# Product-key experts on one core: the gathered block is selected first and its rows are fetched from there, 56 of 128 first products run ahead

## The chip, the cores and the metric

The kernel runs on one core of one Trainium2 chip. A core has a matrix engine (PE, with its weight loads, PEld), a vector engine (DVE), a scalar engine (ACT), a GpSimd engine (POOL) and DMA queues, one of them fed by SyncE (SP). The metric is the device time of one execution in microseconds (us).

## The reference

The program is two transformer blocks over 512 tokens of 1024 features in float32. The part that the change touches is the feed-forward of the first block, with product keys and 16384 experts. Cut to what matters:

```python
def peer_ffn(h, w_query, sub_keys, expert_u, expert_v):
    # per token and head (8 heads): two 128-wide queries
    q = h @ w_query                              # 1024 -> 8 x 2 x 128
    s = q . sub_keys                             # 128 scores for each half
    (v1, i1), (v2, i2) = top16(s[0]), top16(s[1])
    best, pos = top16(v1[:, None] + v2[None, :]) # 16 of the 256 pairs
    gate = softmax(best); expert = i1 * 128 + i2
    # 8 heads x 16 = 128 experts of each token
    y = sum_e gate_e * gelu(h . expert_u[e]) * expert_v[e]
```

## The kernel before, in words

The 512 tokens are four blocks of 128. **Block 0 is gathered**: for each of its 128 (head, pick) slots one indirect DMA from POOL brings the 128 rows of `peer_u` that the 128 tokens picked (`g_row`, 128 x 1024, 512 KB, three buffers), and DVE forms the dot products (L889); then 128 such rows of `peer_v` are added up with the weights `dots` (L894). That makes 256 rows in all. **Blocks 1 to 3 (384 tokens) are dense**: all 16384 experts are computed in 128 chunks of 128. A chunk has a *first product* (`hp`: 24 matmuls 128x384 of `peer_uT`, then a gelu into `act`), a weighting with the gates `gt`, and a *second product* (`o`: 18 matmuls 128x512 with `peer_v`, added up in PSUM over all chunks). Every weight tile is 128x1024 in float32 and goes through `split`: a DMA on SP's queue (`w_raw`), a rounding copy on ACT (`w_hi`) and the difference on DVE or POOL (`w_lo`, L108), with five buffers (`WB`); each product then takes three matmul passes.

The gates of a dense block come in three steps. `scores` multiplies with 16 tiles of `w_query` (24 matmuls 128x256 for a pair of blocks) and with the sub-keys (L735, 128x128 matmuls in float32), and takes the 16 best of 128 for each (`top16`: five DVE operations L745 to L749 with their value loads). `select` finds the 16 best pairs and their expert numbers on DVE (sums `cs`, 16 more `top16` of 50, comparisons of 128x2048 float16 `ge` and `pr`). `gates` turns them into a dense table by matmuls of one-hots: for 16 tokens at a time DVE writes two `onehot` and two `gated` tiles (128x2048 float16, L853, L854, two buffers each) with `TI` tokens innermost, PE multiplies them token by token (L860, L861: 32 matmuls 128x128, whose operands have a stride of `TI` elements), ACT evicts to `stage`, and a DMA stores them in `gd`. One such step of 16 tokens is called a *G step* here; a block has eight.

The order of the program: scores of blocks 2 and 3, scores of blocks 0 and 1, ten first products (`ahead(10)`), then for blocks 2, 3, 1 a `select` and eight G steps, each with one first product behind it until `PRE` = 32 are there; then the `select` of block 0; and then 128 iterations of second products, of which the first 96 (*doubles*) compute one more first product and the last 32 (*singles*) none. The rows of block 0 are fetched in iterations 5 to 119, in proportion to the work of an iteration, each held until the matmuls of the iteration before are done. First products made ahead split on POOL, the others on DVE. A scheduler orders each engine's instructions within these dependences, so the order on an engine differs from the program's text; each engine runs its own list strictly in order.

The second block of the model follows and isn't touched.

Of the kernel before, what the change touches and what calls it, by code (L numbers as in the profile page):

```python
# [32 lines left out]
SKIP = 5  # L33
LAST = 8
PRE = 32
# [3 lines left out]
TI = 4  # L39
# [45 lines left out]
class Body:  # L85
# [516 lines left out]
    def peer(self, gp, er):  # L602

        nc, tc, A = self.nc, self.tc, self.A
        with ExitStack() as es:
            pool = es.enter_context(tc.tile_pool(name="peer", bufs=1, reuse_waits="tile"))
            wpool = es.enter_context(tc.tile_pool(name="w2", bufs=1, reuse_waits="tile"))
            psh = es.enter_context(tc.tile_pool(name="psh", bufs=2, space=PSUM, reuse_waits="tile"))
# [10 lines left out]
            with tc.tile_pool(name="p2a", bufs=1, reuse_waits="tile") as pa:  # L619
                self.normal(hi, lo, pa, psg)  # L620
                er.close()
                pb = eb.enter_context(tc.tile_pool(name="p2b", bufs=1, side="right", reuse_waits="tile"))
                self.select_tables(pb)
                self.scores(hi, lo, tvs, tis, pa, wpool, psm, psg)
            pact = es.enter_context(tc.tile_pool(name="acts", bufs=1, reuse_waits="tile"))
            act = {}

            def first_product(i, eng=None):
# [6 lines left out]
                act[i] = pact.tile([P, TD], F32, name="act", bufs=PRE + 2)  # L635
                nc.scalar.activation(act[i], ps, AF.Gelu)  # L636
# [12 lines left out]
            nc.vector.scalar_tensor_tensor(slots[:, 0], ij[:, 0], float(P), ij[:, 1], op0=OP.mult, op1=OP.add)  # L649
            nc.vector.tensor_copy(slots[:, 1], g)  # L650
            eb.close()
            with ExitStack() as ec:
# [3 lines left out]
                self.x = None  # L656
                rows = self.gather(slots[:, 0], slots[:, 1], pc)
                next(rows)
                pace = [2 if i + PRE < NE else 1 for i in range(NE)]
                for i in range(NE):  # L660
# [3 lines left out]
                    if i + PRE < NE:  # L664
                        first_product(i + PRE)
                    src = A["peer_v"][i * P:(i + 1) * P, :].rearrange("p (r d) -> p r d", r=1)
                    vh, vl = self.split(src, wpool, WB, None, 1)
                    w = act.pop(i)
# [6 lines left out]
                    for b in range(3):  # L675
                        sl = slice(b * P, (b + 1) * P)
                        for s_, m_ in ((wh, vh), (wh, vl), (wl, vh)):
                            for n in range(2):
                                last = nc.tensor.matmul(out[b][n], s_[:, sl], m_[:, n * 512:(n + 1) * 512],  # L679
                                                 start=i == 0 and m_ is vh and s_ is wh,  # L680
                                                 stop=i == NE - 1 and s_ is wl)
                    if i == NE - PRE + 4:
                        self.keep(gp)
                    if SKIP <= i < NE - LAST:
                        rows.send((2 * P * sum(pace[SKIP:i + 1]) // sum(pace[SKIP:NE - LAST]), mm))
                    mm = last
                for b in range(3):
                    for n in range(2):
                        xs = self.x[b + 1][:, n * 512:(n + 1) * 512]
                        nc.vector.tensor_tensor(xs, xs, out[b][n], op=OP.add)  # L690
# [24 lines left out]
    def scores(self, hi, lo, tvs, tis, pool, wpool, psm, psg):  # L715
        nc, A = self.nc, self.A
        sk = pool.tile([P, 16, P], F32, name="skT")
        nc.sync.dma_start(sk, A["sub_keysT"])
        for first in (2, 0):
# [451 lines left out]
```

## Time and profile before

| what | value |
|---|---|
| time, median of 3 runs | 2060.81 us (2060.49 to 2061.16) |
| the profiled execution: its time, its span | 2068.49 us, 2066.7 us |
| PE busy | 1940.7 us, 94% of the span |
| DVE busy | 1428.8 us, 69% |
| ACT busy | 886.0 us, 43% |
| POOL busy | 639.8 us, 31% |
| mean granted clock of PE | 0.973 of full speed |
| DMA | 402.90 MB, 195 GB/s over the span |

Busy time is the union of an engine's instructions. Matmuls are pipelined: a record of one is longer than the distance to the next, so what a matmul costs is read from the starts of successive ones. Times in the rows are microseconds from the start of the span, "mean ns" is that of one instruction, and "x" is a count. The program's stages in this span: first mixers to 410, normalisation to 428, scores to 541, ten first products to 608, gates of three blocks to 817, second products from 833 to 1748, second block to the end.

### The profile page before, as it was taken

What the parts mean: (1) busy time and instruction counts of PE and PEld (TensorE: products, weight loads), DVE (VectorE), ACT (ScalarE), POOL (GpSimd) and SP (SyncE); (2) the same over time, 40 slices, a digit from 0 to 9 for tenths busy, and PEclk for the clock granted to TensorE, in tenths of its full rate; (3) what the DMA queues carried; (4) which work ended last, traced back from release to release, by engine and by line L of the source; (5) the groups of instructions that cost most, each with busy time, mean ns of one, the idle gap of its engine ahead of it and who ended that gap; (6) DMA issues with size and microseconds to landing.
All of it is one profiled execution on the core that took longest, in us unless ns stands there. A gap on an engine that the chain in (4) does not pass through costs nothing.

```text
span 2066.7 us, 30059 instructions
## 1 busy us (share of the span) xinstructions
PE 1940.7 (94%) x11393; PEld 1760.8 (85%) x11393; DVE 1428.8 (69%) x2662; ACT 886.0 (43%) x1373; POOL 639.8 (31%) x459
## 2 busy tenths in 40 slices
PE   7999988998779999999999999999999999999998
PEld 6778777998779899899999999999999777779998
DVE  3486976379998866778777777877778675443563
ACT  4564745254437666333333333333333334343352
POOL 4334233075452230144333434343333341000000
PEclk9999999999899999999999999999999999999999
DMA  4211014354224445999888988988988775342211
GB/s 163 69 62 50 33 42 143 123 164 133 92 92 180 177 163 222 313 314 335 304 306 308 316 310 284 337 315 302 313 297 291 272 270 196 103 136 74 82 62 52
DMA packets 150354, 402.90 MB, mean 195 GB/s; under 512 B 11584, under 2 KB 60736, under 8 KB 147008
## 3 DMA queue, kind: packets, MB, share of 16 engines
q1 hardware_dynamic: 112768, 264.64, 38.2%
q0 software_dynamic: 36864, 134.23, 18.0%
q8 instruction: 89, 1.46, 0.3%
q10 hardware_dynamic: 576, 2.10, 0.3%
q14 instruction: 57, 0.47, 0.1%
HBM read 371.05 MB, written 29.88 MB: 194 GB/s over the span
## 4 chain that ended last, share of the span: by engine, by line
PE 59%; DVE 12%; DMA 5%; issue 3%; POOL 1%; ACT 1%; DVEq 0%; POOLq 0%; ACTq 0%
PE o L679 21%; PE hp L634 7%; PE hp L633 7%; PE hp L632 7%; DMA g_row<-peer_v,idx 3%; PE mm L121 2%; PE mm L122 2%; PE mm L123 2%; PE mm L133 2%; PE mm L132 2%; PE mm L131 2%; DVE gated L854 1%; PE g L860 1%; PE mm L861 1%; PE g L861 1%
## 5 line engine op out<-in xcount | busy, mean ns | idle before, releaser
L107 ACT ACTIVATE w_hi<-w_raw 128x1024 fp32r<-128x1024 f32 x366 | 385.8, 1059 | 576.5 <-PE hp L633 168.8
L108 DVE TENSOR_TENSOR w_lo<-w_raw,w_hi 128x1024 fp32r<-128x1024 f32 x268 | 326.3, 1219 | 101.2 <-ACT w_hi L107 100.8
L632 PE MATMUL hp<-xT_hi,w_hi 128*128 128x384 f32 x1024 | 350.5, 342 | 20.9 <-ACT act L636 20.9
L633 PE MATMUL hp<-xT_lo,w_hi 128*128 128x384 f32 x1024 | 349.3, 341 | 0.0
L634 PE MATMUL hp<-xT_hi,w_lo 128*128 128x384 f32 x1024 | 348.8, 341 | 0.0
L108 POOL TENSOR_TENSOR w_lo<-w_raw,w_hi 128x1024 fp32r<-128x1024 f32 x98 | 244.9, 2508 | 254.0 <-ACT w_hi L107 244.7
L885 POOL DMA_INDIRECT g_row<-peer_u,idx x128 | 170.5, 1332 | 353.5 <-PE o L679 128.9
L885 POOL DMA_INDIRECT g_row<-peer_v,idx x128 | 167.5, 1308 | 266.4 <-PE o L679 139.8
L679 PE MATMUL o<-w_hi,wl 128*128 128x512 f32 x768 | 239.8, 394 | 6.4 <-DVE wl L674 6.4
L679 PE MATMUL o<-w_hi,wh 128*128 128x512 f32 x768 | 240.2, 394 | 2.5 <-ACT wh L673 2.5
L679 PE MATMUL o<-w_lo,wh 128*128 128x512 f32 x768 | 238.9, 392 | 0.0
L889 DVE SCALAR_TENSOR_TENSOR g_row<-g_row,kv 128x1024 f32<-128x1024 f32 x128 | 156.3, 1223 | 95.7 <-DMA g_row<-peer_u,idx 94.9
L632 PEld LDWEIGHTS hp<-xT_hi,w_hi 128*128 128x128 f32 x1024 | 196.1, 191 | 25.1 <-ACT act L636 21.5
L633 PEld LDWEIGHTS hp<-xT_lo,w_hi 128*128 128x128 f32 x1024 | 196.2, 192 | 3.6
L634 PEld LDWEIGHTS hp<-xT_hi,w_lo 128*128 128x128 f32 x1024 | 195.6, 191 | 0.0
L894 DVE SCALAR_TENSOR_TENSOR x<-g_row,dots,x 128x1024 f32<-128x1024 f32 x103 | 132.2, 1284 | 81.3 <-DMA g_row<-peer_v,idx 80.6
L679 PEld LDWEIGHTS o<-w_hi,wl 128*128 128x128 f32 x768 | 144.8, 189 | 39.3 <-DVE wl L674 8.3
L679 PEld LDWEIGHTS o<-w_lo,wh 128*128 128x128 f32 x768 | 145.2, 189 | 32.4
L673 ACT ACTIVATE wh<-act 128x384 fp32r<-128x384 f32 x128 | 67.1, 524 | 243.1 <-PE o L679 234.3
L679 PEld LDWEIGHTS o<-w_hi,wh 128*128 128x128 f32 x768 | 143.9, 189 | 27.1 <-ACT wh L673 2.8
L94 POOL TENSOR_TENSOR rs<-rs_t,mhalf 128x1 f32<-128x1 f32 x20 | 13.8, 688 | 391.2 <-DVE rs_t L93 382.0
L121 PE MATMUL mm<-xT_hi,w_hi 128*128 128x256 f32 (+1 forms) x384 | 128.9, 336 | 0.6 <-ACT xT_hi L158 0.6
(335 smaller groups left out, 4013.7 us busy)
## 6 DMA issues: line engine op xcount, KB each, us to landing
w_raw<-peer_uT SPq DMA_DIRECT2D x128, 512.0 KB
w_raw<-peer_v SPq DMA_DIRECT2D x128, 512.0 KB
w_raw<-w_in SPq DMA_DIRECT2D x54, 512.0 KB
gd<-stage SPq DMA_DIRECT2D x24, 1024.0 KB
gt<-gd SPq DMA_DIRECT2D x16, 1536.0 KB
w_raw<-w_query SPq DMA_DIRECT2D x32, 512.0 KB
w_raw<-w_out SPq DMA_DIRECT2D x16, 512.0 KB
b<-c_b SPq DMA_DIRECT2D x16, 448.0 KB
```

What stands on the lines that cost most here:

```text
L107: nc.scalar.activation(hi[:, sl], raw, AF.Copy)
L108: eng.tensor_tensor(lo[:, sl], raw, hi[:, sl].bitcast(F32), op=OP.subtract)
L121: nc.tensor.matmul(ps, a, xh[:, kc, :], start=kc == 0, stop=False)
L122: nc.tensor.matmul(ps, a, xl[:, kc, :], start=False, stop=False)
L632: nc.tensor.matmul(ps, uh[:, kc, :], hi[:, kc, P:], start=kc == 0, stop=False)
L633: nc.tensor.matmul(ps, uh[:, kc, :], lo[:, kc, P:], start=False, stop=False)
L634: nc.tensor.matmul(ps, ul[:, kc, :], hi[:, kc, P:], start=False, stop=kc == KC - 1)
L673: nc.scalar.activation(wh, w, AF.Copy)
L679: last = nc.tensor.matmul(out[b][n], s_[:, sl], m_[:, n * 512:(n + 1) * 512], start=i == 0 and m_ is vh and s_ is wh, stop=i == NE - 1 and ...
L885: dma = nc.gpsimd.indirect_dma_start(out=u, out_offset=None, in_=A["peer_v" if k >= P else "peer_u"], in_offset=bass.IndirectOffsetOnAxis( ...
L889: nc.vector.scalar_tensor_tensor(u, u, 1.0, self.h2, op0=OP.mult, op1=OP.mult, accum_out=dots[:, c:c + 1])
L894: nc.vector.scalar_tensor_tensor(y, u, dots[:, c:c + 1], x, op0=OP.mult, op1=OP.add)
```

## The change

1. The order: the scores of blocks 0 and 1 come first, then four first products, `select` of block 0, and the gather's set-up. Then come the scores of blocks 2 and 3, with one first product and one row of the gather sent per tile of `w_query`, and `select` of block 1 is called within them. The gates go 1, 2, 3, each G step with one first product and one row; six first products stand ahead of `select` of blocks 2 and 3.
2. First products ahead: 56 instead of 32. The first 32 go to DRAM (`actd`) and are loaded again for the last 32 second products; 24 stay in SBUF. The second products take the chunks in the order 56..127, 32..55, 0..31.
3. Rows: `EARLY` is 56, but 16 + 24 = 40 calls of `row()` send one each. From the second iteration of the second products on the rest are due in proportion, counted from 56, so that the second iteration brings the count from 40 to 58.
4. One-hots: `TI` is 2 instead of 4. A one-hot tile still has 2048 elements and a G step still two of each kind; the stride that PE reads is 4 bytes instead of 8.

```diff
-PRE = 32
+AHEAD = 56
+STAY = 24
+EARLY = 56
-TI = 4
+TI = 2
...
             def ahead(n):
                 for _ in range(n):
-                    if len(act) < PRE:
-                        first_product(len(act), nc.gpsimd)
-            ahead(10)
-            for b in (2, 3, 1):
-                ij, g = self.select(tvs[b], tis[b], pb)
-                self.gates(b - 1, ij, g, pb, [(psg, "g"), (psm, "mm")], pst, ahead)
-            ahead(PRE)
-            ij, g = self.select(tvs[0], tis[0], pb)
+                    i = next(done)
+                    if i >= AHEAD:
+                        return
+                    if i < AHEAD - STAY:
+                        t = pact[0].tile([P, TD], F32, name="actt", bufs=3)
+                        first_product(i, t, nc.gpsimd)
+                        nc.sync.dma_start(self.actd[i], t)
+                    else:
+                        at = 0 if i < AHEAD - 10 else 1
+                        act[i] = pact[at].tile([P, TD], F32, name=f"act{at}", bufs=(STAY - 10, 10)[at])
+                        first_product(i, act[i], nc.gpsimd)
...
+                self.scores(0, hi, lo, tvs, tis, sk, ps, wpool, psm, psg)
+                ahead(4)
+                ij, g = self.select(tvs[0], tis[0], pb)
...
+                rows = self.gather(slots[:, 0], slots[:, 1], prow)
+                next(rows)
+                sent = count(1)
+                def row():
+                    n = next(sent)
+                    if n <= EARLY:
+                        rows.send((n, None))
+                one = {}
+                def between(i):
+                    ahead(1)
+                    row()
+                    if i == 7:
+                        one[1] = self.select(tvs[1], tis[1], pb)
+                self.scores(2, hi, lo, tvs, tis, sk, ps, wpool, psm, psg, between)
...
+            def step():
+                ahead(1)
+                row()
+            for b in range(1, NB):
+                if b > 1:
+                    ahead(6)
+                    one[b] = self.select(tvs[b], tis[b], pb)
+                self.gates(b - 1, *one[b], pb, [(psg, "g"), (psm, "mm")], pst, step)
+            ahead(AHEAD)
...
+                order = [*range(AHEAD, NE), *range(AHEAD - STAY, AHEAD), *range(AHEAD - STAY)]
+                weight = [2 if i >= AHEAD else 1 for i in order]
...
+                    else:
+                        ready[i] = pc.tile([P, TD], F32, name="actr", bufs=3)
+                        nc.sync.dma_start(ready[i], self.actd[i])
...
-                    if SKIP <= i < NE - LAST:
-                        rows.send((2 * P * sum(pace[SKIP:i + 1]) // sum(pace[SKIP:NE - LAST]), mm))
+                    if 0 < n < NE - LAST:
+                        part = (2 * P - EARLY) * sum(weight[1:n + 1]) // sum(weight[1:NE - LAST])
+                        rows.send((EARLY + part, mm))
...
-                for g in range(ng):
+                for t2 in range(0, GB, 4):
...
-                    for t in range(TI):
-                        nc.tensor.matmul(ps[:, t], one[:, ng + g, :, t], two[:, 0, g, :, t], start=True, stop=False)
-                        nc.tensor.matmul(ps[:, t], one[:, ng + g, :, t], two[:, 1, g, :, t], start=False, stop=True)
+                    for t in range(4):
+                        g, r = divmod(t2 + t, TI)
+                        for k in range(2):
+                            nc.tensor.matmul(ps[:, t], one[:, ng + g, :, r], two[:, k, g, :, r], start=k == 0, stop=k == 1)
...
-                self.tc.add_manual_dep(dma.ins, after.ins.name, PACE, reason="rows keep pace with the chunks")
+                if after is not None:
+                    self.tc.add_manual_dep(dma.ins, after.ins.name, PACE, reason="rows keep pace with the chunks")
```

What the scheduler makes of it is seen in the engines' lists. First POOL's list of the changed program, at the place where the first rows stand; `w_lo_5009` is the split of the first `w_query` tile of blocks 2 and 3, and from there splits of `w_query` tiles and of first products alternate:

```order
156 L109 TENSOR_TENSOR w_lo_5132<-w_raw_5133,w_hi_5131 128x1024
157 L109 TENSOR_TENSOR w_lo_5183<-w_raw_5184,w_hi_5182 128x1024
158 L944 DMA g_row_5041<-peer_u,idx_4971 128x1024
159 L944 DMA g_row_5128<-peer_u,idx_4971 128x1024
160 L944 DMA g_row_5215<-peer_u,idx_4971 128x1024
161 L109 TENSOR_TENSOR w_lo_5219<-w_raw_5220,w_hi_5218 128x1024
162 L109 TENSOR_TENSOR w_lo_5270<-w_raw_5271,w_hi_5269 128x1024
163 L944 DMA g_row_5302<-peer_u,idx_4971 128x1024
164 L944 DMA g_row_5389<-peer_u,idx_4971 128x1024
165 L109 TENSOR_TENSOR w_lo_5306<-w_raw_5307,w_hi_5305 128x1024
166 L944 DMA g_row_5476<-peer_u,idx_4971 128x1024
167 L944 DMA g_row_5563<-peer_u,idx_4971 128x1024
```

It goes on in this way until all 40 early rows have been asked for, also those that the text sends from the G steps: they stand among some 20 splits of the scores of blocks 2 and 3, and none stands among the splits of the G steps. In the list before, the rows came after POOL's last split:

```order
194 L108 TENSOR_TENSOR w_lo_7891<-w_raw_7892,w_hi_7890 128x1024
195 L108 TENSOR_TENSOR w_lo_7974<-w_raw_7975,w_hi_7973 128x1024
196 L885 DMA g_row_8600<-peer_u,idx_8223 128x1024
197 L885 DMA g_row_8603<-peer_u,idx_8223 128x1024
198 L885 DMA g_row_8668<-peer_u,idx_8223 128x1024
199 L885 DMA g_row_8671<-peer_u,idx_8223 128x1024
```

Next, DVE's list of the changed program between the gates of block 1 and those of block 2. `ge_8433` and `pr_8443` belong to the `select` of block 3, `onehot_7483` is the first one-hot of block 2:

```order
1181 L872 TENSOR_TENSOR ge_8433<-pf_8431,t_row_3924 128x2048
1182 L873 TENSOR_TENSOR pr_8443<-pr_8443,ge_8433 128x2048
1183 L823 TENSOR_TENSOR pr_8443<-pr_8443 128x8x128
1184 L823 TENSOR_TENSOR pr_8443<-pr_8443 128x8x64
1185 L823 TENSOR_TENSOR pr_8443<-pr_8443 128x8x32
1186 L824 TENSOR_TENSOR ij_8435<-pr_8443 128x128
1187 L896 CAST ijT_7476<-tp_7472 128x16x8 x2
1188 L897 TENSOR_SCALAR gT_7477<-tp_7472 128x16x8
1189 L912 TENSOR_TENSOR onehot_7483<-t_iota_3923,ijT_7476 128x2048
```

So what is left of `select` of block 2 and the whole `select` of block 3 stand between the one-hots of blocks 1 and 2. PE's list has seven first products there, seven more between the gates of blocks 2 and 3, and seven within the gates of each block (before: 8 within those of the first and of the second block, 6.9 within the third's). Last, DVE's list at the start of the second products:

```order
1271 L109 TENSOR_TENSOR w_lo_9496<-w_raw_9497,w_hi_9495 128x1024
1272 L949 SCALAR_TENSOR_TENSOR g_row_9340,dots_4973<-g_row_9340,kv_3805 128x1024
1273 L949 SCALAR_TENSOR_TENSOR g_row_9343,dots_4973<-g_row_9343,kv_3805 128x1024
1274 L109 TENSOR_TENSOR w_lo_9532<-w_raw_9533,w_hi_9531 128x1024
1275 L949 SCALAR_TENSOR_TENSOR g_row_9346,dots_4973<-g_row_9346,kv_3805 128x1024
1276 L949 SCALAR_TENSOR_TENSOR g_row_9349,dots_4973<-g_row_9349,kv_3805 128x1024
1277 L727 TENSOR_TENSOR actf_9394<-actf_9394,gt_9214 128x384
1278 L949 SCALAR_TENSOR_TENSOR g_row_9352,dots_4973<-g_row_9352,kv_3805 128x1024
1279 L731 TENSOR_TENSOR wl_9503<-actf_9394,wh_9502 128x384
1280 L109 TENSOR_TENSOR w_lo_9564<-w_raw_9565,w_hi_9563 128x1024
```

It goes on in this way: the 18 rows of the second iteration (`g_row_9340` to `g_row_9391`) stand among seven splits; before, two or three rows stood between two pairs of splits.

PE's list has 95.1 first products behind the last matmul of the gates before the change (3.1 of them ahead of the first second product), and 73.0 after it (4.4).

## Rows read from the trace of the kernel before

**Rows 1.** The page: busy time, share of the span, instructions.

```profile
PE 1940.7 (94%) x11393; PEld 1760.8 (85%) x11393; DVE 1428.8 (69%) x2662; ACT 886.0 (43%) x1373; POOL 639.8 (31%) x459
```

**Rows 2.** Windows: length, busy PE, PEld, DVE, ACT, POOL, PE clock, DMA share, GB/s.

```profile
480.00:815.00 335.00, 290.84 (x1959) 282.57 (x1958) 295.77 (x765) 182.41 (x222) 111.65 (x43) 0.91 0.41 149
835.00:1560.00 725.00, 725.00 (x3664) 658.65 (x3664) 548.99 (x718) 256.89 (x350) 277.85 (x210) 1.00 0.90 310
```

**Rows 3.** Windows of the first products and of the gates of three blocks, same columns.

```profile
541.00:608.00 67.00, 46.11 (x243) 45.19 (x242) 66.90 (x302) 23.43 (x29) 26.25 (x10) 0.85 0.24 79
608.00:681.60 73.60, 66.65 (x453) 64.07 (x452) 65.78 (x108) 48.26 (x53) 21.50 (x8) 0.93 0.46 170
681.60:753.50 71.90, 66.87 (x453) 64.70 (x452) 53.81 (x49) 46.35 (x52) 19.48 (x8) 0.93 0.49 181
753.50:817.20 63.70, 61.16 (x425) 59.00 (x424) 48.28 (x41) 39.42 (x45) 6.75 (x2) 0.95 0.48 180
```

**Rows 4.** Timeline of PE in the gates: start, length, instruction.

```profile
650.17 0.30 PE L861 MATMUL g<-gated,onehot 128*128 128x128 f16 x1
...
651.83 0.29 PE L861 MATMUL mm<-gated,onehot 128*128 128x128 f16 x1
...
654.39 0.34 PE L634 MATMUL hp<-xT_hi,w_lo 128*128 128x384 f32 x1
...
657.51 0.34 PE L634 MATMUL hp<-xT_hi,w_lo 128*128 128x384 f32 x1
```

**Rows 5.** Timeline of PE in the scores, from sub-key matmuls to the next ones.

```profile
428.27 0.61 PE L735 MATMUL g<-skT,pqT 128*128 128x128 f32 x4
428.64 0.37 PE L121 MATMUL mm<-xT_hi,w_hi 128*128 128x256 f32 x1
...
431.57 0.61 PE L735 MATMUL g<-skT,pqT 128*128 128x128 f32 x4
...
434.84 0.61 PE L735 MATMUL g<-skT,pqT 128*128 128x128 f32 x4
```

**Rows 6.** Groups of DVE, 480 to 815: count, busy us, mean ns, idle before.

```profile
L853 DVE TENSOR_TENSOR onehot<-t_iota,ijT 128x2048 f16<-128x2048 f16 x48 | 72.7, 1527 | 26.0 <-PE mm L861 25.9
L854 DVE TENSOR_TENSOR gated<-onehot,gT 128x2048 f16<-128x2048 f16 x48 | 67.5, 1444 | 0.0
L749 DVE FIND_INDEX8 ti<-tv,rest 128x8 uint32<-128x128 f32 x34 | 9.6, 282 | 0.0
L108 DVE TENSOR_TENSOR w_lo<-w_raw,w_hi 128x1024 fp32r<-128x1024 f32 x5 | 6.1, 1223 | 2.9 <-ACT w_hi L107 2.9
```

**Rows 7.** Timeline of DVE in the gates of the second block.

```profile
686.39 1.21 DVE L853 TENSOR_TENSOR onehot<-t_iota,ijT 128x2048 f16<-128x2048 f16 x1
687.52 3.36 DVE L854 TENSOR_TENSOR gated<-onehot,gT 128x2048 f16<-128x2048 f16 x1
```

**Rows 8.** Timeline of POOL at the same place.

```profile
687.35 2.45 POOL L108 TENSOR_TENSOR w_lo<-w_raw,w_hi 128x1024 fp32r<-128x1024 f32 x1 [2.16 <-ACT w_hi L107]
```

**Rows 9.** Groups of POOL, 480 to 815.

```profile
L108 POOL TENSOR_TENSOR w_lo<-w_raw,w_hi 128x1024 fp32r<-128x1024 f32 x43 | 112.0, 2610 | 172.4 <-ACT w_hi L107 166.6 <-PE hp L634 5.9
```

**Rows 10.** Groups of POOL, 835 to 1560.

```profile
L885 POOL DMA_INDIRECT g_row<-peer_u,idx x128 | 170.5, 1332 | 353.5 <-PE o L679 128.9 <-DMA w_raw<-peer_v 97.9 <-DVE g_row L889 58.6
```

**Rows 11.** Timeline of POOL and of DVE in a double: a row asked for, its use.

```profile
1199.53 0.95 POOL L885 DMA_INDIRECT g_row<-peer_u,idx  x1 [5.51 <-PE o L679]
...
1205.15 1.22 DVE L889 SCALAR_TENSOR_TENSOR g_row<-g_row,kv 128x1024 f32<-128x1024 f32 x1 [2.26 <-DMA g_row<-peer_u,idx]
1206.31 0.08 DVE L889 DVE_READ_ACCUMULATOR g_row<-g_row,kv 128x1 f32 x1
```

**Rows 12.** PE's waits in the second products, 833 to 1755: total, times, longest.

```profile
PE o L679 <- DVE wl L674: 6.4, 4, 3.9
PE o L679 <- ACT wh L673: 2.5, 1, 2.5
```

**Rows 13.** ACT's roundings of weights in singles: count, durations, first and last start.

```profile
L673 ACT ACTIVATE wh<-act x28: 525/525/529, 1632.4 to 1746.0; 128x384 fp32r<-128x384 f32 x28
```

More of the change, by code (lines that the diff above doesn't have):

```diff
@@ L620, in peer, with first_product @@
                 self.normal(hi, lo, pa, psg)
[L621 to L628, printed above, removed]
+            er.close()
+            pb = eb.enter_context(tc.tile_pool(name="p2b", bufs=1, side="right", reuse_waits="tile"))
+            self.select_tables(pb)
+            pact = [es.enter_context(tc.tile_pool(name="acts", bufs=1, reuse_waits="tile"))]
+            act, done = {}, count()
+            def first_product(i, out, eng=None):
                 uh, ul = (t.rearrange("p (k f) -> p k f", k=KC) for t in self.split(A["peer_uT"][i], wpool, WB, eng, 1))
@@ L655, in peer, with prepare @@
                 out = [[pso.tile([P, 512], F32, name=f"o{b}{n}") for n in range(2)] for b in range(3)]
[L656 to L660, printed above, removed]
+                self.x0 = pc.tile([P, D], F32, name="x0")
+                nc.sync.dma_start(self.x0, self.x1[0])
+                order = [*range(AHEAD, NE), *range(AHEAD - STAY, AHEAD), *range(AHEAD - STAY)]
+                weight = [2 if i >= AHEAD else 1 for i in order]
+                ready = {}
+                def prepare(n):
+                    if n >= NE:
+                        return
+                    i = order[n]
+                    if i >= AHEAD:
+                        ready[i] = pc.tile([P, TD], F32, name="actf", bufs=3)
+                        first_product(i, ready[i])
+                    elif i in act:
+                        ready[i] = act.pop(i)
+                    else:
+                        ready[i] = pc.tile([P, TD], F32, name="actr", bufs=3)
+                        nc.sync.dma_start(ready[i], self.actd[i])
+                prepare(0)
+                for n, i in enumerate(order):
                     if i % GR == 0:
@@ L713, in normal, with scores @@
         nc.gpsimd.tensor_tensor(self.h2, rows[0], gf, op=OP.mult)
[L715 removed]
+    def scores(self, first, hi, lo, tvs, tis, sk, pool, wpool, psm, psg, between=None):
         nc, A = self.nc, self.A
[L717 to L740 removed]
@@ new lines, in scores, with late @@
+        tokens = slice(first * P, first * P + 256)
+        xt = (hi[:, :, tokens], lo[:, :, tokens])
+        late = None
+        for i in range(16):
+            w = [t.rearrange("p (k f) -> p k f", k=KC) for t in self.split(A["w_query"][i], wpool, WB, nc.gpsimd, 1)]
+            qT = pool.tile([P, 256], F32, name="pqT", bufs=2)
+            ps = psm.tile([P, 512], F32, name="mm")
+            self.mm_feat(ps[:, :256], w, xt, 0)
+            nc.scalar.activation(qT, ps[:, :256], AF.Copy)
+            if late:
+                late()
+            def late(i=i, qT=qT):
+                ps = psg.tile([P, 512], F32, name="g")
+                for b in range(2):
+                    nc.tensor.matmul(ps[:, b * P:(b + 1) * P], qT[:, b * P:(b + 1) * P], sk[:, i, :], start=True, stop=True)
+                sc = pool.tile([P, 2, P], F32, name="sc", bufs=4)
+                nc.scalar.activation(sc, ps[:, :256].rearrange("p (a n) -> p a n", a=2), AF.Copy)
+                for b in range(2):
+                    self.top16(tvs[first + b][:, i], tis[first + b][:, i], sc[:, b, :], pool, P)
+            if between:
+                between(i)
@@ L742, in top16 @@
+        late()
     def top16(self, v, n, src, pool, width):
@@ L823, in select, with gates @@
         return out.rearrange("p n h k -> p n (h k)"), g.rearrange("p h k -> p (h k)")
-    def gates(self, n, ij, g, pool, psums, pst, ahead):
+    def gates(self, n, ij, g, pool, psums, pst, step):
         nc = self.nc
```

63 lines of the change are left out of this document (23 added, 40 removed).

## Prediction

> **What bounds the kernel now.** I read the page first: PE is busy for 94% of the span [rows 1], so the question is where its other 6% lie and whether the change reaches them. The windows by stage answer that. During the second products PE is busy all the time, 725.00 of 725 us, and DVE is not (549 us) [rows 2]: there only taking work away from PE helps. From 480 to 815, while the gates are made, PE is busy for 291 of 335 us at a granted clock of 0.91, and DVE for 296 [rows 2]. The finer windows show who waits for whom: from 541 to 608 DVE is busy for 66.9 of 67 us with the selections, and PE has only ten first products to do (46 us) [rows 3]; in the three blocks of gates PE is busy for 61 to 67 us of 64 to 74, DVE for 48 to 66 [rows 3]. So this is a stage that DVE paces first and PE afterwards, and a stage that PE paces alone. The change moves PE work from the second into the first, and DVE and POOL work (40 rows of the gather) too. The first helps only so far as PE would have waited; the second can hurt, since DVE is the engine that was late.
>
> **What leaves the second products.** PE's list has 95.1 first products behind the last gate before, 73.0 after: 22.1 leave. Eighteen pitches of the first product's matmuls take 657.51 - 654.39 = 3.12 us [rows 4], so one takes 24 x 0.1733 = 4.16 us, and 22.1 take **-92 us**.
>
> **The scores and the rows.** A tile of `w_query` with its sub-key matmuls takes 434.84 - 431.57 = 3.27 us [rows 5]. Sixteen from 428.3 end at 480.6, and four first products end at 497. Then come 16 steps of one tile and one first product, 7.43 us each: 616 if PE never waits. Two things could make it wait.
>
> The selection of block 0 must be ready for the first row. DVE's 295.8 us from 480 to 815 [rows 2] hold the one-hots (72.7 + 67.5), five splits (6.1) [rows 6], 32 `top16` of 128 (five operations of 0.28 us, 1.4 us each [rows 6], 45 together) and four selections: (295.8 - 146.3 - 45) / 4 = 26 us each. So the block is selected at about 482 + 26 = 508, and POOL asks for rows from 509. By then it has split for two and a half of the steps, which lasts PE until 515; the next split stands behind three requests only, and that is in time.
>
> From there on POOL's list has 40 rows and 20 splits for ten steps of PE. A split takes POOL 2.61 us [rows 9], a request 1.33 us [rows 10]: 52 + 53 = 105 us, where PE needs 74. So POOL paces these ten steps; they end at 509 + 105 = 614 and not at 590, and the last three and a half at 640 and not at 616. PE loses 24 us. The bounds: with the shortest request in the rows, 0.95 us [rows 11], POOL needs 90 us and PE loses 9; at the other end the rows' turns add to the splits. A row is used 5.62 us after it is asked for, and 1.3 us later its buffer is free [rows 11]: 6.9 us, with three buffers 2.3 us for a row, 40 x 2.3 + 52 = 144 us, and PE loses 63. I take POOL's sum, since splits and transfers run at the same time.
>
> **The one-hots.** DVE's work stays: two one-hots and two gated tiles for 16 tokens, 2048 elements each. What can change is PE's reading. Now a matmul of the gates follows the next after (651.83 - 650.17) / 14 = 0.119 us [rows 4]. The nearest row with contiguous operands is that of the sub-keys: four passes in 428.64 - 428.27, 0.0925 us each [rows 5]. I take that value: 0.026 us less for each of 768 matmuls, 20 us in all and 6.7 for a block. The bounds are no gain and 0.051 us, which is what 128 columns more cost a matmul (384 columns 0.173, 256 columns (431.57 - 428.64) / 24 = 0.122 [rows 4, 5]). The Trainium skill ("SBUF — State Buffer", section "Specifications (TRN2)") says that SBUF is read in lines of 16 bytes and that two hits on a line are enough for the full rate. No run here shows it; by that rule a stride of 8 bytes has its two hits already, 4 bytes would bring nothing, and the sum would be 20 us higher.
>
> A block of gates took 71.9 us with eight first products and 63.7 with 6.9 [rows 3]. It now has seven: 71.9 - 4.2 - 6.7 = 61 and 63.7 - 6.7 + 0.4 = 57; I take **59 us**. DVE alone would need 8 x 4 x 1.21 [rows 7] = 39 us, and more where POOL splits beside it: a gated tile that began while a split ran took 3.36 us and ended 1.1 us behind it [rows 7, 8]. With seven such waits of some 2 us it has 53 us, and stays just below PE. The same page of the Trainium skill, section "SBUF: two separate sides", has this as a lock: a DVE operation with two SBUF inputs and a POOL operation that reads SBUF exclude each other. The trace agrees (3.36 us and not 1.21); by that rule a block can't be shorter than 39 + 7 x 2.6 = 57 us, however fast PE's reading becomes.
>
> **Between the blocks.** DVE's list has what is left of one selection and the whole of another ahead of the one-hots of block 2. That is 52 us less what ran before, some 8 (the sums `cs` and the first of its eight `top16` sets stand among the one-hots of block 1), and DVE begins about 6 us before PE ends the block; transposes and the first one-hot add 3: 41 us, of which seven first products cover 29. PE waits 12 us. Between blocks 2 and 3 DVE has nothing to do, and PE spends 29 + 3 = 32 us.
>
> The last gate then ends at 640 + 59 + 41 + 59 + 32 + 59 = **890 us**, and not at 817 [rows 3]: **+73 us**. PE without any wait would have it at 616 + 3 x (7 x 4.16 + 256 x 0.0925) + 2 x 29 = 833, so the stage still loses some 57 us, against the 44 us of idle time that it had [rows 2].
>
> **The second products.** PE waited 6.4 + 2.5 us here [rows 12], late, in the stretch where singles begin. Rows per single fall from 1.24 to 1.05 (198 rows over the weights of iterations 2 to 119), so I take half of it off: **-4**. But the second iteration sends 18 rows at once. Three in flight at 2.3 us make 41 us; DVE needs 18 x 1.31 + 7 x 1.22 + 7 x 1.1 = 40 us, and PE passes these seven splits in 29 us. Splits stand between the rows in DVE's list, so PE is short of 12 us less what the buffers have ahead, which may be all of it: 0 to 12, I take **+8**. The reloaded chunks add 192 KB to each of the last 24 singles that still fetch rows: 512 + 192 + 192 (gates) + 537 KB in the 4.21 us of a single ((1746.0 - 1632.4) / 27 [rows 13]) is 348 GB/s (of 1024 bytes to the KB); 310 GB/s went with a DMA share of 0.90 [rows 2], which makes 344 the most. So these singles are 1% short, 1 us in 24 of them, and have no slack for a late transfer: **+3**. The stores of 32 x 192 KB lie in a stage with a DMA share under 0.5 [rows 3] and cost nothing; if they were not covered, no instruction of PE waits for them either.
>
> **Sum.** -92 + 73 - 4 + 8 + 3 = **-12 us** on the profiled execution's 2068.5 us. The median of the runs shown is 2060.8, 0.4% less; the difference carries over: **2049 us**.
>
> **Rivals.** *The rows hold up POOL (slower).* POOL runs its list in order: the next request waits until DVE has used the row three before, and DVE has `top16` sets and the rest of the selection of block 1 between the rows; the splits behind the request wait as well, and PE with them. For it: DVE had no idle time just here (66.9 of 67 us [rows 3]). Against it: `top16` is short and hardly blocks. At its full price, 63 us instead of 24, the time is 2049 + 39 = 2088; it decides the sign when the scores end after 652, at half a microsecond more for each early row than POOL's own 1.33, and at half its price the time is 2069.
>
> *The one-hots don't gain from the shorter stride:* +20 us, 2069. Against it is the pitch of 0.0925; for it, that those operands differ from the one-hots in their type too. The rule of the lines of 16 bytes would have it so.
>
> *DVE writes one-hots more slowly with two tokens innermost.* The float16 tile of 2048 takes 1.21 us [rows 7], a float32 one of 1024 takes 1.22 [rows 6]; if the shorter inner run halved the rate, 96 operations would cost 1.2 us more, 115 us, of which PE's margin covers little: 2150. Nothing in the trace speaks for it.
>
> *PE never waits.* If splits and requests overlap better, the selections are covered by first products and a gate matmul falls to 0.08 us, the last gate ends near 860: 2019.
>
> **How the numbers follow.** What a measurement of this kernel can tell from no change is about 0.2%, 4 us. The forecast has 42%, PE hardly waiting 8%: faster 50%. The rows in POOL's list have 21%, the stride without effect 12%, slow one-hots 4%: slower 37%. For the remaining 13% the terms cancel, since +73 and -85 are near each other. The likeliest case by itself spans 2033 to 2056. For 8 in 10 the range goes down to 2015 and, with the rows at nearly full price, up to 2086.
>
> **What would show it.** In the profile of the changed kernel: the last gate matmul at about 890 (break-even at about 902); the last tile of `w_query` near 640 with POOL busy almost all the time from 509 to 614; gate matmuls at 0.09 us; a wait of some 12 us of PE for a one-hot's transposes ahead of block 2; a short wait for `w_lo` in the first iterations of the second products, and PE busy all the time behind it. The prediction is wrong if the scores end past 652, if a block of gates takes 65 us or more, or if PE waits in the singles for reloaded chunks.

## The result: 4.6% slower

The changed kernel takes 2156.6 us (median of 4 runs, 2151.2 to 2160.8) against 2061.0 of the kernel before: ratio 1.0458, 95% interval 1.0427 to 1.0489. Forecast was 2049 us, so the sign was wrong and the time lies outside the range. The profiled execution has a span of 2151.4 us, 84.7 more than before.

The page of the changed kernel shows that PE was busy for as long as before (1937.7 us, 1940.7 before [rows 1]), so that the added time is time without work on PE:

```profile
PE 1937.7 (90%) x11393; PEld 1738.3 (81%) x11393; DVE 1429.3 (66%) x2638; ACT 882.1 (41%) x1375; POOL 717.5 (33%) x483
```

But an equal busy time isn't an equal pace. The faster gate matmuls alone, in the kernel before, bring PE's busy time down to 1903.6 us (`e4_before_ti2` below). The changed kernel has them too, and its busy time is 34 us longer than that, at a mean granted clock of 0.962 of full speed (0.973 before).

Where it waits is seen in windows of the changed kernel, cut at the ends of its stages (columns as in [rows 2]):

```profile
490.00:670.00 180.00, 140.77 (x860) 137.20 (x859) 149.60 (x452) 64.05 (x94) 136.09 (x74) 0.90 0.70 230
667.50:727.80 60.30, 49.55 (x430) 46.62 (x428) 56.90 (x122) 38.42 (x47) 38.19 (x9) 0.94 0.61 224
727.80:767.10 39.30, 32.01 (x171) 31.34 (x169) 38.99 (x129) 22.51 (x24) 18.67 (x6) 0.91 0.41 133
767.10:831.00 63.90, 50.02 (x429) 47.42 (x427) 57.74 (x42) 39.56 (x48) 23.49 (x9) 0.89 0.50 182
831.00:860.20 29.20, 29.20 (x172) 29.17 (x170) 0.00 (x0) 11.28 (x15) 15.68 (x7) 1.00 0.43 147
860.20:916.70 56.50, 48.77 (x429) 46.91 (x427) 50.39 (x40) 37.86 (x45) 12.58 (x4) 0.94 0.54 200
936.40:1110.00 173.60, 149.34 (x692) 130.24 (x693) 115.42 (x168) 48.69 (x67) 62.54 (x51) 0.92 0.85 281
1110.00:1500.00 390.00, 383.54 (x1932) 345.86 (x1931) 272.37 (x319) 132.94 (x185) 123.55 (x97) 1.00 0.82 275
1500.00:1590.00 90.00, 70.02 (x315) 60.12 (x314) 59.84 (x77) 22.07 (x31) 31.69 (x17) 0.91 0.81 269
1590.00:1700.00 110.00, 109.09 (x480) 89.43 (x479) 77.66 (x83) 40.09 (x54) 32.84 (x27) 1.00 0.81 281
1700.00:1841.00 141.00, 128.38 (x540) 102.44 (x538) 96.21 (x117) 45.03 (x62) 34.28 (x26) 0.98 0.84 281
```

The first row is the scores with their rows of the gather, then come the gates of block 1, the gap with two selections, the gates of block 2, the gap with DVE idle (0.00), the gates of block 3, and the second products from 936 to 1841. The blocks and gaps (60, 39, 64, 29, 57 us) are near the forecast's 59, 41, 59, 32, 59. The scores are not: PE waits for 39 of 180 us, at a granted clock of 0.90. And the second products, where PE was busy for 725 of 725 us [rows 2], now lose time at three places: 24 us from 936 to 1110, 20 us from 1500 to 1590, 13 us behind 1700, and 6 between.

The last gate matmul starts at 916.7 (817.2 before, forecast 890): +99.5 us. From there to the last second product it takes 1840.9 - 916.7 = 924 us, and took 1754.5 - 817.2 = 937: 13 us gained where the forecast had 85. This second miss, 72 us, is the greater one. It has two parts, as windows of this stage before and now show:

```profile
817.20:1755.00 937.80, 928.48 (x4590) 831.05 (x4587) 689.15 (x868) 333.44 (x454) 339.84 (x258) 0.99 0.87 299
916.70:1841.00 924.30, 858.81 (x4060) 746.20 (x4057) 626.93 (x767) 298.08 (x409) 284.89 (x218) 0.97 0.83 278
```

PE's idle time rose from 9 to 65 us. Its busy time fell by 70 us, though 92 us of work had left: 22 us came back while the granted clock fell from 0.99 to 0.97. PE's timeline of the changed kernel shows how the two hang together:

```profile
1033.36 1.22 PE L736 MATMUL o<-w_hi,wh 128*128 128x512 f32 x2 [5.59 <-ACT wh L730]
1034.38 1.05 PE L736 MATMUL o<-w_lo,wh 128*128 128x512 f32 x2
1035.23 1.05 PE L736 MATMUL o<-w_hi,wl 128*128 128x512 f32 x2
1036.09 1.05 PE L736 MATMUL o<-w_hi,wh 128*128 128x512 f32 x2
1036.94 0.97 PE L736 MATMUL o<-w_lo,wh 128*128 128x512 f32 x2
1037.76 0.63 PE L736 MATMUL o<-w_hi,wl 128*128 128x512 f32 x2
1038.23 0.62 PE L736 MATMUL o<-w_hi,wh 128*128 128x512 f32 x2
```

After a wait of 5.59 us the next pairs of matmuls follow each other after 0.82 to 1.02 us, at a granted clock of 0.53 from 1033 to 1038 (near 1.2 GHz, the lower of the two levels). Only then it is 0.47 us again, at the full 2.4 GHz. This wait cost some 2 us more than its own length.

PE's waits of the changed kernel in that stage name their source (total, times, longest):

```profile
PE o L736 <- ACT wh L730: 44.8, 20, 7.7
PE o L736 <- DVE wl L731: 20.4, 13, 3.7
```

`wh` is a chunk's weighted activations after rounding, and `wl` is what the rounding left over; the same two waits were 2.5 and 6.4 us [rows 12]. What `wh` itself waited for, before and now, is the row on which the explanation rests. ACT's waits of the kernel before, 835 to 1560:

```profile
ACT wh L673 <- PE o L679: 136.2, 65, 3.7
```

and of the changed kernel, 936 to 1590:

```profile
ACT wh L730 <- DVE actf L727: 345.5, 69, 14.1
```

Before, ACT had the chunk's weighted activations ready and waited until PE had freed the buffer of `wh`: the chain was ahead of PE. Now it waits for DVE's weighting, 69 times, for 345 us: the chain is behind. (ACT has time to spare; 45 us of this reached PE.) The first product of a chunk used to be computed 32 iterations ahead of its second product and kept in the ring of tiles `act`; in the changed kernel's loop the call `prepare(n + 1)` computes it one iteration ahead. Between the two lie now a gelu, the weighting on DVE, the rounding on ACT and its rest on DVE, and DVE's list is in order, with uses of rows in it, each of which waits for a transfer. That was theory C of the experiments. Its rivals: the burst of 18 rows (theory A), late splits, tables of gates loaded in a crowd where the doubles end (theory G), and the rows of the singles (theory S).

### The profile page after: what moved, and what is told of

The parts are those of the page before. It is cut to its first block, busy times and chain, and to the rows that moved or that the text cites. A ratio compares the mean times of both kernels' runs of the same rounds, so it can differ in the third digit from the quotient of the medians.

```text
span 2151.4 us, 29974 instructions
## 1 busy us (share of the span) xinstructions
PE 1937.7 (90%) x11393; PEld 1738.3 (81%) x11393; DVE 1429.3 (66%) x2638; ACT 882.1 (41%) x1375; POOL 717.5 (33%) x483
## 4 chain that ended last, share of the span: by engine, by line
PE 29%; DMA 21%; DVE 18%; issue 15%; POOL 4%; ACT 2%; POOLq 0%; DVEq 0%; SPq 0%; ACTq 0%
DMA g_row<-peer_v,idx 8%; DMA g_row<-peer_u,idx 6%; PE o L736 5%; PE mm L132 3%; PE mm L134 3%; PE mm L133 3%; DVE g_row L949 2%; POOL g_row L944 2%; PE mm L122 2%; PE mm L123 2%; PE mm L124 2%; PE hp L633 2%; PE hp L634 2%; PE hp L635 2%; DMA actr<-actd 2%
## 5 line engine op out<-in xcount | busy, mean ns | idle before, releaser
L109 POOL TENSOR_TENSOR w_lo<-w_raw,w_hi 128x1024 fp32r<-128x1024 f32 x122 | 327.5, 2693 | 209.5 <-ACT w_hi L108 189.1
L109 DVE TENSOR_TENSOR w_lo<-w_raw,w_hi 128x1024 fp32r<-128x1024 f32 x244 | 297.7, 1222 | 108.9 <-ACT w_hi L108 108.5
L944 POOL DMA_INDIRECT g_row<-peer_v,idx x128 | 172.7, 1349 | 373.0 <-PE o L736 256.8
L736 PE MATMUL o<-w_hi,wh 128*128 128x512 f32 x768 | 247.6, 404 | 44.9 <-ACT wh L730 44.8
L736 PE MATMUL o<-w_hi,wl 128*128 128x512 f32 x768 | 245.4, 401 | 20.5 <-DVE wl L731 20.4
L944 POOL DMA_INDIRECT g_row<-peer_u,idx x128 | 163.1, 1274 | 294.7 <-PE o L736 202.0
L949 DVE SCALAR_TENSOR_TENSOR g_row<-g_row,kv 128x1024 f32<-128x1024 f32 x128 | 171.2, 1344 | 104.8 <-DMA g_row<-peer_u,idx 100.2
L730 ACT ACTIVATE wh<-actf 128x384 fp32r<-128x384 f32 x72 | 37.9, 526 | 354.1 <-DVE actf L727 345.5
L954 DVE SCALAR_TENSOR_TENSOR x<-g_row,dots,x 128x1024 f32<-128x1024 f32 x81 | 104.0, 1284 | 76.1 <-DMA g_row<-peer_v,idx 75.9
L124 PE MATMUL mm<-xT_hi,w_lo 128*128 128x256 f32 (+1 forms) x384 | 125.2, 326 | 7.0 <-POOL w_lo L109 7.0
```

What stands on the lines that cost most here:

```text
L109: eng.tensor_tensor(lo[:, sl], raw, hi[:, sl].bitcast(F32), op=OP.subtract)
L124: nc.tensor.matmul(ps, b, xh[:, kc, :], start=False, stop=kc == KC - 1)
L736: last = nc.tensor.matmul(out[b][h], s_[:, sl], m_[:, h * 512:(h + 1) * 512], start=n == 0 and m_ is vh and s_ is wh, stop=n == NE - 1 and ...
L944: dma = nc.gpsimd.indirect_dma_start(out=u, out_offset=None, in_=A["peer_v" if k >= P else "peer_u"], in_offset=bass.IndirectOffsetOnAxis( ...
L949: nc.vector.scalar_tensor_tensor(u, u, 1.0, self.h2, op0=OP.mult, op1=OP.mult, accum_out=dots[:, c:c + 1])
L954: nc.vector.scalar_tensor_tensor(y, u, dots[:, c:c + 1], x, op0=OP.mult, op1=OP.add)
```

## The experiments

Each kernel ran beside the kernel before on one chip; its ratio goes by those runs. The changed kernel has 1.0458.

**Rows sent evenly** (`e1_spread`):

```diff
-EARLY = 56
+EARLY = 40
```

> The changed kernel with EARLY = 40: the second iteration of the second products sends two rows instead of 18. Theory A (a row that lands late holds DVE's list, the splits behind it and PE): the loss of some 33 us between 936 and 1110 goes, PE busy over 95% there, time 2120 to 2132 us. Rival B (the first iterations are short of DMA or of splits whatever the rows do): within 8 us of the changed kernel's 2157.

2139.2 us, ratio 1.0382 (1.0347 to 1.0416): 16 us less than the changed kernel. In its windows PE waits for 6 us from the first second product to 1110, not 24, but for 11 from 1110 to 1500:

```profile
939.80:1110.00 170.20, 164.05 (x807) 145.69 (x808) 117.34 (x165) 55.82 (x77) 57.53 (x45) 0.99 0.84 281
1110.00:1500.00 390.00, 378.64 (x1893) 338.08 (x1892) 276.06 (x330) 129.10 (x181) 130.33 (x102) 1.00 0.85 284
1500.00:1590.00 90.00, 76.63 (x339) 64.39 (x339) 64.32 (x81) 26.48 (x38) 26.32 (x20) 0.92 0.89 304
```

So the burst is one cause, worth 16 us where theory A had expected 25 to 37. The stalls in the steady doubles are not its doing.

**No rows with the scores** (`e2_norows`): `EARLY = 0`.

> The changed kernel with EARLY = 0: all 256 rows go with the second products, none with the scores. Theory A: the scores of blocks 2 and 3 end near 620 and not at 667, the last gate matmul near 870 and not at 917, and the burst of 18 rows is gone: 2070 to 2090 us. Rival B (the scores are slow because POOL and DVE have the splits, selections and top16 anyway): scores end after 650, time over 2110.

2128.3 us, ratio 1.0326 (1.0294 to 1.0359). The first half of the expectation came out within 4 us: the groups of sub-key matmuls and of gate matmuls (count, durations, first and last start) end at 623.8 and 872.0, 44 and 45 us earlier than in the changed kernel.

```profile
L791 PE MATMUL g<-skT,pqT x128: 271/275/580, 427.9 to 623.8; 128*128 128x128 f32 x128
L921 PE MATMUL mm<-gated,onehot x384: 218/218/312, 631.8 to 872.0; 128*128 128x128 f16 x192
```

So the rows held the scores up, by 44 us, not splits or selections. The time as a whole missed the expectation by some 40 us: with 256 rows in them the second products lost 67 us to the two waits instead of 65, though the burst was gone, and from the last gate matmul to their end they took 933 us instead of 924. So the 40 rows weren't cheap there either.

**One-hots by four tokens in the changed kernel** (`e3_ti4`): `TI = 4`.

> The changed kernel with one-hots by four tokens again (TI = 4). Gate matmuls go back from 0.06 to 0.119 us, 43 us more of PE in three blocks. If PE paces the blocks of gates: the last gate 35 to 43 us later, 2190 to 2200 us. If DVE paces them (my walk: DVE 53 us a block, PE 44): 10 to 25 us later, 2167 to 2182 us.

2170.3 us, ratio 1.0517 (1.0489 to 1.0544): 0.6%, 12 us, more than the changed kernel. In the traces its last gate matmul starts 27 us later (943.7), just above the 10 to 25 expected if DVE paces the blocks and below the 35 to 43 if PE does, and the second products took 917 us instead of 924. So DVE paces most of a block, as the walk had it.

**One-hots by two tokens in the kernel before** (`e4_before_ti2`), the loop over `t2` of the change and `TI = 2`, nothing else:

> The kernel before with one-hots by two tokens alone. Gate matmuls 0.06 us instead of 0.119, 43 us less of PE. DVE has 54 and 48 us of work in the second and third block, 66 in the first: these bound the blocks, which took 73.6, 71.9 and 63.7: 8 + 14 + 13 = 35 us at most; with the waits for one-hots that stay 15 to 35 us, so 2026 to 2046 us.

2044.7 us, ratio **0.9907** (0.9881 to 0.9934). The last gate matmul starts at 797.4 and not at 817.2, a gain of 20 us at the lower end of the expected 15 to 35. PE's line on its page:

```profile
PE 1903.6 (93%) x11393; PEld 1721.9 (84%) x11393; DVE 1433.1 (70%) x2662; ACT 883.3 (43%) x1373; POOL 663.6 (32%) x459
```

This one part of the change beats both kernels.

**Tables of gates paced** (`e6_gt_spread`), with EARLY = 40:

```diff
-                        nc.sync.dma_start(gt, ...)
+                        load = nc.sync.dma_start(gt, ...)
+                        if n >= GR:
+                            self.tc.add_manual_dep(load.ins, ends[n - 6].ins.name, PACE, ...)
```

> EARLY = 40 as in e1_spread (2139 us), and the load of each table of gates but the first waits for the second products six iterations earlier. Theory G (where the doubles end, DVE weights the kept chunks at once, which frees tables, so that five tables of 1.5 MB are loaded in 90 us and rows and splits come late): the stall around the end of the doubles, 16 us in e1_spread from 1500 to 1620, mostly goes: 2118 to 2130. If those waits have another cause: within 6 us of 2139.

Ratio 1.0385 (1.0368 to 1.0403), the same as `e1_spread`. Theory G fell: the crowd of table loads is there in the changed kernel's trace (five in 90 us), but without it nothing gets faster.

**A lead of four** (`e7_lead4`; the tiles `actr` of the reloaded chunks get six buffers too):

```diff
-                        ready[i] = pc.tile([P, TD], F32, name="actf", bufs=3)
+                        ready[i] = pc.tile([P, TD], F32, name="actf", bufs=6)
...
-                prepare(0)
+                for m in range(4):
+                    prepare(m)
...
-                    prepare(n + 1)
+                    prepare(n + 4)
```

> The changed kernel with first products four iterations ahead of their second product and not one (four more float32 tiles of 128x384). Theory C (before, a chunk's weighting had 32 iterations of lead; now gelu, weighting on DVE, rounding on ACT and its rest on DVE lie between the first product and the second of the next iteration, so each row that DVE waits for holds PE): the waits of PE for the weights' rounding and rest in the doubles, some 50 of 84 us of idle time, mostly go: 2105 to 2125. If late splits are what PE waits for, lead changes nothing: within 8 us of 2157.

2128.4 us, ratio 1.0313 (1.0295 to 1.0332): 30 us less, just short of the expected 32 to 52. From its last gate matmul (922.5) to the end of the second products it takes 890 us, and the changed kernel 924. Its windows show where:

```profile
950.00:1110.00 160.00, 147.74 (x723) 131.03 (x722) 115.00 (x168) 50.36 (x69) 65.56 (x51) 0.97 0.88 305
1110.00:1500.00 390.00, 390.00 (x1978) 354.91 (x1977) 276.57 (x339) 139.03 (x190) 137.89 (x100) 1.00 0.85 287
1500.00:1590.00 90.00, 66.98 (x288) 54.80 (x287) 59.15 (x70) 22.29 (x31) 30.91 (x20) 0.91 0.84 285
```

From 1110 to 1500 PE is busy for 390.00 of 390 us again, and ACT's `wh` waits for PE as it did before:

```profile
ACT wh L731 <- PE o L737: 101.0, 45, 2.4
```

What is left is the burst (12 us ahead of 1110) and the stretch where the doubles end (23 us). The edit gives the splits no more lead over their products, so late splits are not what the doubles waited for.

**Lead and even rows** (`e9_lead4_spread`), and **both with paced tables** (`e8_lead4_gt_spread`):

> EARLY = 40 and a lead of four, tables not paced. Theory C: 25 to 35 us below e1_spread's 2139, so 2104 to 2114, and the rest of the idle time at the end of the doubles. If splits are what PE waits for: 2131 to 2147.

> All three together: EARLY = 40, lead of four, tables of gates paced. If theories C and G and the burst are the whole loss of the second products, PE's idle time there falls from 84 us to under 20 and the time to 2075 to 2092. If the rows themselves or DMA hold PE, it stays over 2105.

Ratios 1.0241 (1.0216 to 1.0267) and 1.0240 (1.0223 to 1.0257). The two repairs add up (-0.75% and -1.45% alone, -2.2% together), and the tables again do nothing. `e9`, at 2118.3 us, lies 4 us above its expected range, and `e8`, at 2114.4, missed the expected 2092 by 22. PE has hardly any waits in the doubles (3 of 500 us), as the first of three windows of `e9_lead4_spread` shows; the 56 iterations without a first product keep theirs:

```profile
1000.00:1500.00 500.00, 497.18 (x2519) 451.80 (x2517) 359.65 (x463) 174.74 (x240) 185.64 (x134) 1.00 0.86 292
1500.00:1600.00 100.00, 80.87 (x319) 64.81 (x319) 73.50 (x83) 28.12 (x37) 38.05 (x26) 0.90 0.88 300
1600.00:1800.00 200.00, 185.11 (x781) 149.61 (x780) 141.79 (x161) 67.38 (x88) 53.71 (x43) 0.97 0.85 285
```

**Fewer rows in the singles**, `e10_weights` with 4 to 1 and `e13_w20` with 20 to 1 instead of 2 to 1, on top of `e9_lead4_spread`:

```diff
-                weight = [2 if i >= AHEAD else 1 for i in order]
+                weight = [20 if i >= AHEAD else 1 for i in order]
```

> EARLY = 40, lead of four as in e9_lead4_spread (ratio 1.024 to the kernel before), and rows shared out 4 to 1 between doubles and singles instead of 2 to 1: 2.6 per double, 0.65 per single. Theory S (what is left of the loss lies in the 56 singles, 34 to 40 us of idle time there, since a single wants 512 KB of weights, 192 of gates, 192 of reload and a row in 4.1 us, and DVE's list waits for late rows): PE's idle time in the singles falls below 20 us, time 15 to 25 us less, ratio 1.012 to 1.017. If the reloads or the order of the end are the cause: within 0.3% of 1.024.

> As e9_lead4_spread and e10_weights with rows shared out 20 to 1: 2.9 per double and 7 rows in all the singles. If rows hold the singles (theory S): from 1600 on PE idles under 5 us and around the end of the doubles less than 20 us; the doubles may wait, since DVE has 7.3 of 8.3 us and DMA 335 GB/s there; ratio 1.012 to 1.022. If the reloads or the loads of the second block's inputs hold them: idle time in the singles stays at some 25 us as in e10_weights.

`e10_weights`: 1.0223 (1.0195 to 1.0250), no difference from `e9_lead4_spread` that can be told, where theory S had expected 1.012 to 1.017. `e13_w20`: 1.0404 (1.0373 to 1.0435), much slower than its expected 1.012 to 1.022. A form with no rows at all in the singles (`e13_doubles`) gave no result. The three windows of `e13_w20` show what the singles gained and the doubles lost:

```profile
1000.00:1500.00 500.00, 480.32 (x2377) 430.23 (x2376) 384.43 (x470) 159.95 (x225) 202.14 (x166) 0.98 0.91 314
1500.00:1600.00 100.00, 73.65 (x300) 60.59 (x299) 70.72 (x81) 24.71 (x33) 46.01 (x27) 0.86 0.87 300
1600.00:1800.00 200.00, 195.21 (x859) 160.45 (x858) 110.32 (x141) 72.89 (x96) 7.85 (x7) 1.00 0.64 201
```

With seven rows in all the singles PE loses 5 of 200 us there and not 15, with the same reloads: it is the rows that hold the singles for these 10 us. But the doubles have no room for them: they lose 20 us of 500 at a DMA share of 0.91. The dip from 1500 to 1600 stays (26 us).

**The loads for the second block later** (`e14_keep_late`), at iteration 112 and not 76:

> As e9_lead4_spread (ratio 1.024), with the loads of x and of the memory's keys and values (2 MB) 36 iterations later, at iteration 112. If they are what makes the dip of some 20 us between 1480 and 1600: ratio 1.012 to 1.017. If not: 1.021 to 1.027.

1.0241 (1.0217 to 1.0266): no effect. What makes the dip where the doubles end is still open; tables and these loads are not it. The chain of waits that ended last in the changed kernel from 1490 to 1592 says what was late there:

```profile
by line: DMA g_row<-peer_v,idx 50.8%; issue 30.9%; DMA gt<-gd 11.6%; DVE x L954 7.8%; DVE act L727 2.4%; DVE w_lo L109 2.3%; DVE actf L727 1.0%; POOL g_row L944 0.5%; DVE wl L731 0.5%; POOLq L944 0.1%; DVEq L954 0.0%
1559.67 15.15 DMA g_row<-peer_v,idx
```

Half of it is rows on their way, one of them for 15 us from its request on, where a row in a double of the kernel before was used 5.6 us after it was asked for [rows 11]. Why they are slow there, no run tells.

**Lead of four and no rows with the scores** (`e11_lead4_norows`):

> Lead of four and EARLY = 0 (all 256 rows with the second products). The last gate at 872 as in e2_norows, 45 us earlier than in the changed kernel; the 40 rows more cost DVE and DMA in a stage that has them free in the doubles but not in the singles. By theory S: doubles without waits, singles with some 10 us more than e9_lead4_spread: 35 us less than its 2118, ratio 1.005 to 1.010. If early rows save in the second products as much as they cost before: ratio 1.020 to 1.028.

2087.7 us, ratio 1.0111 (1.0080 to 1.0142), just above the 1.005 to 1.010 of the first expectation. It is the best form of the new order that ran, and still behind the kernel before, though its one-hots are the faster ones. Its last gate is at 875.7, 58 us later than before, where 92 us of first products were moved ahead of it; the gain of 34 us is lost again in the second products: PE waits for `wl` and `w_lo` for 48 us (9 for `wl` and `wh` before [rows 12]), and its busy time falls by 78 us there and not by 92.

**More first products ahead in the kernel before** (`e12_before_pre35`), with `TI = 2`, and with one spare tile in the ring `act` instead of two:

```diff
-PRE = 32
+PRE = 35
...
-            ahead(10)
+            ahead(14)
```

> The kernel before with one-hots by two tokens (e4_before_ti2, 2045 us) and 35 first products ahead, 14 of them instead of ten before the first gates, where PE had 21 us of idle time in 67. Three first products leave the second products, 12.5 us, and lie in that idle time: 2030 to 2036 us. If DVE's selections are slowed by the additional splits on POOL: 2040 to 2047.

2047.7 us, ratio 0.9927 (0.9903 to 0.9950): not faster than `e4_before_ti2`, and at the upper end of the range expected if DVE's selections are slowed. The last gate matmul starts 8 us later (805.3), and PE has a new wait of 12.5 us for the first `wh`. Work moved ahead was given back there; what the missing spare tile has to do with it, no run tells.

## Why the prediction was wrong, by its steps

**The moved work: right.** Behind the last gate matmul PE has 1752 matmuls of first products (73.0 of 24 each), and had 2283 before (95.1).

**The scores: mis-sized, 27 us.** They end at 667.5, forecast 640, with 652 named as the point that decides the sign; this is the rival "the rows hold up POOL", with 51 us of loss against 24 taken and 63 as the upper bound. The 40 requests and the 24 splits among them took POOL from 510.6 to 652.1, 141 us and not the 105 of POOL's own sum; it was busy for 112 of them. Windows of the changed kernel show who was late, first DVE with the selections, then POOL:

```profile
515.00:575.00 60.00, 42.77 (x263) 42.36 (x264) 59.46 (x138) 22.81 (x32) 44.26 (x24) 0.86 0.71 233
575.00:667.00 92.00, 70.54 (x413) 67.79 (x413) 62.20 (x200) 25.96 (x43) 77.72 (x43) 0.89 0.79 260
```

For the first 60 us DVE is busy for 59.46, and POOL, whose next request needs a buffer that DVE has used, for 44; in the next 92 us POOL is busy for 78. The step that failed is the choice of POOL's own sum as the price "since splits and transfers run at the same time". `e2_norows` confirms the rows as the cause (44 us); that they cost it through DVE's list is read from these windows, and no run separates it. Of the 51 us PE was idle for 39; the rest goes with the lower clock.

**The one-hots: right in sign, larger than taken.** Gate matmuls follow each other after 0.058 us (the last section has the rows); the forecast was 0.0925, with 0.051 as the lower bound. The blocks came out at 60, 64 and 57 us, forecast 59, but not for the forecast's reason: it had PE pace them, and with these matmuls PE alone would need 7 x 4.16 + 256 x 0.058 = 44 us. DVE paces them (50 to 58 us busy in each), so that the number came out near by luck, and the faster matmuls are worth only 12 us of the time here (`e3_ti4`) and 19 in the kernel before. The lock between DVE and POOL that the Trainium skill ("SBUF — State Buffer", section "SBUF: two separate sides") describes agrees with this: block 3 has four splits on POOL beside its one-hots, block 2 nine, and their DVE time is 50 and 58 us for the same work.

**Between the blocks: right**, 39 and 29 us, forecast 41 and 32; DVE is idle in the second.

**The second products: the step that failed.** The forecast gave them +8 for the burst, +3 for the singles and -4 for the late wait, on the ground that PE had waited for next to nothing there before. It read "PE 725.00 of 725" as a property of the stage. It was a property of the 32 iterations of lead, which hid DVE's waits for rows (152 us of them in the kernel before, 835 to 1560, by the waits of DVE there):

```profile
DVE g_row L889 <- DMA g_row<-peer_u,idx: 94.9, 66, 5.9
DVE x L894 <- DMA g_row<-peer_v,idx: 57.5, 34, 5.2
```

DVE waited for rows no longer than that in the changed kernel (146 us from 936 to 1590), but now PE waited with it; a lead of four was enough to end that in the doubles (`e7_lead4`). The changed kernel's loop has `prepare(n + 1)` plainly, and the prediction put this edit at nothing without asking what had hidden the waits. Nor had it a term for the 22 us of the 72 that went with the lower clock. The measured parts, by the ratios and with what the clock cost in each: the lead 30 us, the burst 16 us (+8 taken), together 45. In the singles, where the forecast had +3, `e9_lead4_spread` keeps some 34 us of idle time from 1500 to 1800 (19 + 15), of which 10 are shown to be the rows; the dip of 19 is open.

The chances had 37% for slower, and none of the rivals reached 2157 by the mechanism that was found.

## What to carry to other kernels

Before a stage that never waits is counted on, ask what gives it its slack: the distance between producing and using a tile is such a thing, and cutting the lead from 32 iterations to one let late transfers in an in-order list reach the matrix engine; a lead of four took 30 us of that back (`e7_lead4`). A wait of that engine can cost more than its length, since the granted clock was lower behind it (0.53 behind one of 5.59 us). Work moved out of a full stage brings only what the receiving stage has free: PE was idle for 44 us there [rows 2], and 92 us of first products moved into it delayed its end by 55 us (`e2_norows`) with no early rows and with the faster gate matmuls. Run the parts of a change by themselves; here one of four parts alone brought 0.9%, and all four together cost 4.6%.

## What the runs showed of the hardware that was not expected

With a stride of 4 bytes instead of 8 in both operands, the gate matmuls (128x128 float16, each with its weight load) follow each other after half the time. In PE's timeline of the changed kernel eight stand between 880.24 and 880.70, 0.058 us each (0.119 before [rows 4]):

```profile
880.24 0.62 PE L921 MATMUL g<-gated,onehot 128*128 128x128 f16 x8
880.70 0.62 PE L921 MATMUL mm<-gated,onehot 128*128 128x128 f16 x8
```

The loop that was rewritten with it isn't the cause: with a stride of 8 bytes in the new loop (`e3_ti4`) a weight load is recorded with 117 ns and a matmul with 298, and in the changed kernel with 97 and 218. By the rule weighed in the prediction (the Trainium skill, "SBUF — State Buffer", section "Specifications (TRN2)": two hits on a line of 16 bytes are enough for the full rate) the shorter stride would have made no difference. By this measurement two float16 values on a line weren't enough here; whether the moving operand or the weights make it, no run tells.

A request for a row by POOL can itself take long: in the changed kernel 1.0 us at the median for the rows of `peer_u`, and up to 6.4 for those of `peer_v`. The requests that took 5.0, 4.3 and 6.4 us start at 1514, 1537 and 1560, within the dip where the doubles end; why, no run tells.

```profile
L944 POOL DMA_INDIRECT g_row<-peer_u,idx x128: 934/1045/1977, 510.6 to 1256.3; - x128
L944 POOL DMA_INDIRECT g_row<-peer_v,idx x128: 935/1202/6377, 1258.4 to 1802.4; - x128
```
